# 44 runs of zero products at 22 distances between the addresses of the two operands, in place of thirteen forms

## The chip, the cores and the metric

The kernel runs on one core of one Trainium2 chip. The metric is the device time of one execution in microseconds (us); a nanosecond is written ns. The engines are called as the profile calls them: PE is TensorE's matmul side and PEld its weight loads, DVE is VectorE, ACT ScalarE, POOL GpSimd and SP SyncE. SBUF is the memory that the engines read, PSUM the one that PE writes, in banks of 512 fp32 columns on 128 partitions.

## The reference

Two networks in sequence work on 256 tokens of width 1024: first two layers of a modulated block (feed-forward, a mixer of neighbourhood attention and pooling, feed-forward) with a context stream beside them, then four layers of a second kind (a gated linear attention, a latent attention, a convolution and again the gated one, each followed by a squared-relu MLP and a gated per-layer term). Cut to what the end of the kernel computes:

```python
def second_block(x, p, ...):
    for i in range(DEPTH_2):
        ...
        x = layer_norm(ALPHA * x + h, ln_g[i, 0], ln_b[i, 0])
        x = layer_norm(ALPHA * x + sq_relu_mlp(x, mlp_w1[i], mlp_w2[i]), ln_g[i, 1], ln_b[i, 1])
        x = x + jax.nn.sigmoid(x @ ple_w_gate[i]) * (p[i] @ ple_w_proj[i])
    return x
```

The output is x, 1 x 256 x 1024 fp32. The probe, which is what the change rewrites, is no part of the reference: it multiplies zeros by zeros and its products are read by nobody.

## The kernel before, in words

`_program` builds a `Net` and calls `block1`, `block2` and `probe` one after the other; a scheduler then puts the instructions of each engine in an order, and waits on semaphores tie the engines together. Every weight is loaded once by SP's queue, split by ACT (L169, the rounded part `whi`, type fp32r) and DVE (L170, the rest, `wlo`), and each product is made of three matmuls into one PSUM bank: high by high (L180), high by low (L181, L182), so PE runs long sequences of matmuls of 512 or 256 columns. A matmul in the program is two instructions on PE: the load of the 128 x 128 weights (LDWEIGHTS, shown as PEld) and the matmul that streams the other operand past them.

The last stage of the network is `ple` in its last call. It multiplies x by the gate weights (tiles named `ple`, 128 x 512), ACT takes the sigmoid (L922, tile `sgm`), DVE multiplies by the projected term (L923) and adds into the rows (L924, tile `xr`), both in pieces of 256 columns, and SP sends each piece out (L926).

`probe` comes last in the program. It opens a pool of SBUF tiles and a pool of six PSUM banks. Four fp32r tiles `pra`, `prb`, `prc`, `pre` and two bf16 tiles `pru`, `prv`, each 128 x 1056, are set to zero by DVE (L1288). A helper `run` then issues n matmuls of one form into one bank or two (L1296), as one accumulation: the first starts it, the last ends it. There are thirteen forms, 276 matmuls: p0 to p3 shift either operand by 8 columns (32 bytes), p4 and p10 are bf16, p5 has 256 columns, p6 has 64 columns of weights, p7 two banks, p8 64 rows, p9 the two halves of the rows in turn, and p11 and p12 (24 each) go round two pairs of tiles and several places in each.

The pool takes memory that tiles of the network used before. So the memsets wait for the last readers of that memory, and the banks for the last readers of the banks. Waits follow the part of a tile that an instruction touches: a matmul waits for the memset of what it reads.

Of the kernel before, what the change touches and what calls it, by code (L numbers as in the profile page):

```python
# [8 lines left out]
F32 = mybir.dt.float32  # L9
F32R = mybir.dt.float32r  # L10
I32 = mybir.dt.int32
BF16 = mybir.dt.bfloat16
# [3 lines left out]
PSUM = bass.MemoryType.PSUM  # L16
DRAM = bass.MemoryType.DRAM

P = 128
# [79 lines left out]
class Net:  # L99
# [35 lines left out]
    def bank(self):  # L135
        return self.ps.tile([P, 512], F32, tag="bank", name=self.ph)
# [1140 lines left out]
    def probe(self):  # L1277

        nc = self.nc
        self.ph = "probe"  # L1280
        with ExitStack() as ctx:
            pool = lambda name, bufs, **k: ctx.enter_context(self.tc.tile_pool(name=name, bufs=bufs, **k))
            pp = pool("probe", 1)
            ps = pool("probe_ps", 6, space=PSUM)
            a, b, c, e = (pp.tile([P, 1056], F32R, name="pr" + n) for n in "abce")
            u, v = (pp.tile([P, 1056], BF16, name="pr" + n) for n in "uv")
            for t in (a, b, c, e, u, v):
                nc.vector.memset(t.bitcast(F32) if t.dtype == F32R else t, 0.0)  # L1288
            bank = lambda: ps.tile([P, 512], F32, tag="probe", name="probe")

            def run(name, n, lhs, rhs, out=None, banks=1):
                bs = [bank() for _ in range(banks)]
                for i in range(n):
                    o = bs[i % banks]
                    o = o if out is None else out(o)
                    nc.tensor.matmul(o, lhsT=lhs(i), rhs=rhs(i), start=i < banks, stop=i >= n - banks)  # L1296

            run("p0", 20, lambda i: a[:, 0:128], lambda i: c[:, 0:512])
            run("p1", 20, lambda i: a[:, 0:128], lambda i: c[:, 8:520])
            run("p2", 20, lambda i: a[:, 8:136], lambda i: c[:, 8:520])  # L1300
            run("p3", 20, lambda i: a[:, 8:136], lambda i: c[:, 0:512])
            run("p4", 20, lambda i: u[:, 0:128], lambda i: v[:, 0:512])
            run("p5", 24, lambda i: a[:, 8:136], lambda i: c[:, 8:264], out=lambda o: o[:, :256])
            run("p6", 20, lambda i: a[:, 8:72], lambda i: c[:, 8:520], out=lambda o: o[:64, :])
            run("p7", 20, lambda i: a[:, 0:128], lambda i: c[:, 0:512], banks=2)
            run("p8", 20, lambda i: a[:64, 0:128], lambda i: c[:64, 0:512])
            run("p9", 20, lambda i: a[64 * (i % 2):64 * (i % 2) + 64, 0:128],
                lambda i: c[64 * (i % 2):64 * (i % 2) + 64, 0:512], banks=2)
            run("p10", 24, lambda i: u[:, 0:128], lambda i: v[:, 0:256], out=lambda o: o[:, :256])
            run("p11", 24, lambda i: (a, b)[i % 2][:, 128 * (i % 8):128 * (i % 8) + 128],  # L1310
                lambda i: (c, e)[i % 2][:, 512 * (i // 2 % 2):512 * (i // 2 % 2) + 512])
            run("p12", 24, lambda i: (a, b)[i % 2][:, 8 + 128 * (i % 8):8 + 128 * (i % 8) + 128],
                lambda i: (c, e)[i % 2][:, 8 + 512 * (i // 2 % 2):8 + 512 * (i // 2 % 2) + 512])


_NAMES = [
# [40 lines left out]
```

## Time and profile before

| | us |
|---|---|
| median of the two timed runs | 3102.1 |
| lowest and highest of them | 3097.98, 3106.21 |
| the profiled execution, its own time | 3095.24 |
| its span, first to last instruction | 3093.5 |
| mean granted clock of TensorE in it | 0.997 of full |

The profile is of one execution. An engine's busy share counts its instructions and not its waits. A matmul's duration runs from its start to its modelled end; matmuls overlap in the pipeline, so a stretch of n of them is shorter than n durations. In a row of the timeline, equal instructions that follow each other are merged into one with their count; the duration is then from the first start to the last end. A few per cent of the matmul records can be missing.

### The profile page before, as it was taken

The page shows a single profiled execution, that of the slowest core. Times are in us where ns is not written, and L with a number is a line of the kernel's source. Part 1 is how long each engine was busy: PE and PEld are TensorE (multiplying, and loading weights), DVE is VectorE, ACT ScalarE, POOL GpSimd, SP SyncE. Part 2 cuts the span into 40 slices and gives each one's busy share as a digit, 9 for nine tenths or more (in the row PEclk, how much of TensorE's full clock was granted, in tenths as well). Part 3 has the DMA queues.
Part 4 walks back from the last instruction along what each step waited for, and adds up shares of the span by engine and source line. Part 5 has one row for each costly group of instructions (what it writes and reads, how often), then busy time and mean ns, then how long its engine had stood idle before and what let it go on. Part 6 is the DMA issues. An engine that isn't in the chain of part 4 may idle for free.

```text
span 3093.5 us, 41224 instructions
## 1 busy us (share of the span) xinstructions
PE 3028.1 (98%) x16637; PEld 2518.3 (81%) x16638; DVE 1880.7 (61%) x2460; ACT 1281.8 (41%) x1876; POOL 288.6 (9%) x480
## 2 busy tenths in 40 slices
PE   7999999999999999999999999999999999999999
PEld 5777777787778877877699779887988998788987
DVE  5657665577553875337755577566756765666651
ACT  3222235542222422225644555455544454465440
POOL 2101020010100200011100130010000000021000
PEclk9999999999999999999999999999999999999999
DMA  7545531345442454222446536553655565535550
GB/s 277 188 159 192 169 116 52 103 163 186 152 140 95 164 187 150 93 95 94 138 159 199 191 111 201 188 175 118 198 188 188 179 205 191 175 131 186 188 171 14
DMA packets 321939, 484.75 MB, mean 157 GB/s; under 512 B 16606, under 2 KB 199442, under 8 KB 320340
## 3 DMA queue, kind: packets, MB, share of 16 engines
q1 hardware_dynamic: 307844, 461.75, 45.3%
q0 software_dynamic: 9296, 16.16, 1.6%
q10 hardware_dynamic: 4608, 4.20, 0.5%
q8 instruction: 131, 2.15, 0.3%
q14 instruction: 60, 0.49, 0.0%
HBM read 480.97 MB, written 1.10 MB: 156 GB/s over the span
## 4 chain that ended last, share of the span: by engine, by line
PE 88%; DVE 5%; POOL 2%; ACT 2%; DMA 2%; issue 1%; SPq 0%; ACTq 0%; DVEq 0%; POOLq 0%
PE ffn_gu L180 9%; PE ffn_gu L182 9%; PE ffn_gu L181 9%; PE mlp L181 7%; PE mlp L182 7%; PE mlp L180 7%; PE ffn_dn L182 4%; PE ffn_dn L181 4%; PE ffn_dn L180 4%; PE m L180 2%; PE m L181 2%; PE m L182 2%; PE probe L1296 2%; DVE wlo L170 2%; PE mix_in L181 1%; PE mix_in L180 1%
## 5 line engine op out<-in xcount | busy, mean ns | idle before, releaser
L170 DVE TENSOR_TENSOR wlo<-raw,whi 128x1024 fp32r<-128x1024 f32 (+1 forms) x735 | 884.6, 1211 | 635.9 <-ACT whi L169 620.7
L169 ACT CAST whi<-raw 128x1024 fp32r<-128x1024 f32 (+1 forms) x735 | 760.8, 1038 | 1128.1 <-PE ffn_gu L181 292.9
L181 PE MATMUL ffn_gu<-hT_lo,whi 128*128 128x512 f32 (+1 forms) x1472 | 524.9, 357 | 1.8 <-DVE hT_lo L175 1.8
L180 PE MATMUL ffn_gu<-hT_hi,whi 128*128 128x512 f32 (+1 forms) x1472 | 525.0, 357 | 0.5 <-ACT hT_hi L174 0.5
L182 PE MATMUL ffn_gu<-hT_hi,wlo 128*128 128x512 f32 (+1 forms) x1472 | 524.2, 357 | 0.7 <-DVE wlo L170 0.7
L180 PEld LDWEIGHTS ffn_gu<-hT_hi,whi 128*128 128x128 f32 x1472 | 277.8, 189 | 52.9 <-ACT whi L169 4.2
L181 PEld LDWEIGHTS ffn_gu<-hT_lo,whi 128*128 128x128 f32 x1472 | 277.8, 189 | 43.9 <-DVE hT_lo L175 2.4
L182 PEld LDWEIGHTS ffn_gu<-hT_hi,wlo 128*128 128x128 f32 x1472 | 277.8, 189 | 43.9 <-DVE wlo L170 1.3
L347 DVE SCALAR_TENSOR_TENSOR macc<-raw,sil,macc 128x1024 f32<-128x1024 f32 x224 | 274.6, 1277 | 37.8 <-DMA raw<-in_w_mod_dram 37.8
L180 PE MATMUL mlp<-xT_hi,whi 128*128 128x256 f32 x896 | 253.9, 283 | 0.0
L181 PE MATMUL mlp<-xT_lo,whi 128*128 128x256 f32 x896 | 253.8, 283 | 0.0
L182 PE MATMUL mlp<-xT_hi,wlo 128*128 128x256 f32 x896 | 253.5, 283 | 0.0
L180 PE MATMUL ffn_dn<-whi,hid_hi 128*128 128x512 f32 x616 | 244.1, 396 | 0.0
L181 PE MATMUL ffn_dn<-wlo,hid_hi 128*128 128x512 f32 x616 | 243.6, 395 | 0.0
L182 PE MATMUL ffn_dn<-whi,hid_lo 128*128 128x512 f32 x616 | 243.5, 395 | 0.0
L180 PE MATMUL mlp<-whi,mlp_hi 128*128 128x512 f32 x512 | 199.2, 389 | 0.0
L181 PE MATMUL mlp<-wlo,mlp_hi 128*128 128x512 f32 x512 | 199.2, 389 | 0.0
L182 PE MATMUL mlp<-whi,mlp_lo 128*128 128x512 f32 x512 | 199.2, 389 | 0.0
L181 PEld LDWEIGHTS mlp<-xT_lo,whi 128*128 128x128 f32 x896 | 172.0, 192 | 0.0
L182 PEld LDWEIGHTS mlp<-xT_hi,wlo 128*128 128x128 f32 x896 | 172.0, 192 | 0.0
L180 PEld LDWEIGHTS mlp<-xT_hi,whi 128*128 128x128 f32 x896 | 172.0, 192 | 0.0
L180 PEld LDWEIGHTS ffn_dn<-whi,hid_hi 128*128 128x128 f32 x616 | 115.9, 188 | 29.4 <-ACT yrow L489 2.5
(414 smaller groups left out, 4889.8 us busy)
## 6 DMA issues: line engine op xcount, KB each, us to landing
raw<-in_mlp_w_dram SPq DMA_DIRECT2D x128, 1024.0 KB, 5.3
raw<-in_w_ffn_gate_up_dram SPq DMA_DIRECT2D x80, 1024.0 KB, 5.4
raw<-in_w_mod_dram SPq DMA_DIRECT2D x72, 1024.0 KB, 5.0
raw<-in_w_ffn_down_dram SPq DMA_DIRECT2D x32, 1024.0 KB, 5.1
raw<-in_gla_w_in_dram SPq DMA_DIRECT2D x24, 1024.0 KB, 5.2
raw<-in_w_in_dram SPq DMA_DIRECT2D x16, 1024.0 KB, 5.1
raw<-in_ple_w_gate_dram SPq DMA_DIRECT2D x16, 1024.0 KB, 5.1
raw<-in_w_ffn_down_dram SPq DMA_DIRECT2D x16, 768.0 KB, 4.6
```

The source lines that it names most:

```text
L169: self.nc.scalar.copy(hi, v)
L170: self.nc.vector.tensor_sub(lo, v, hi.bitcast(F32))
L180: mm(ps, lhsT=a[0], rhs=b[0], start=first, stop=False)
L181: mm(ps, lhsT=a[0], rhs=b[1], start=False, stop=False)
L182: mm(ps, lhsT=a[1], rhs=b[0], start=False, stop=last)
L347: nc.vector.scalar_tensor_tensor(acc[s], raw[:, k - k0, :], c, acc[s], ALU.mult, ALU.add)
L1296: nc.tensor.matmul(o, lhsT=lhs(i), rhs=rhs(i), start=i < banks, stop=i >= n - banks)
```

## The change

The body of `probe` is replaced. There is one fp32r tile `pra` of 128 x 26624 (106,496 bytes in each partition), set to zero by 13 memsets of 2048 columns, and a pool of four PSUM banks. The weights are always columns 0 to 127. The other operand begins 4096 + d bytes behind the beginning of the weights, for 22 values of d from 0 to 98304. At each d there is a run of 18 matmuls of 512 columns and a run of 20 matmuls of 256, each run one accumulation in a bank of its own, taken from the four in turn: 44 runs, 836 matmuls.

```diff
-            ps = pool("probe_ps", 6, space=PSUM)
-            a, b, c, e = (pp.tile([P, 1056], F32R, name="pr" + n) for n in "abce")
-            u, v = (pp.tile([P, 1056], BF16, name="pr" + n) for n in "uv")
-            for t in (a, b, c, e, u, v):
-                nc.vector.memset(t.bitcast(F32) if t.dtype == F32R else t, 0.0)
...
-            run("p0", 20, lambda i: a[:, 0:128], lambda i: c[:, 0:512])
...
-            run("p12", 24, lambda i: (a, b)[i % 2][:, 8 + 128 * (i % 8):8 + 128 * (i % 8) + 128],
-                lambda i: (c, e)[i % 2][:, 8 + 512 * (i // 2 % 2):8 + 512 * (i // 2 % 2) + 512])
+            ps = pool("probe_ps", 4, space=PSUM)
+            a = pp.tile([P, 26624], F32R, name="pra")
+            for o in range(0, 26624, 2048):
+                nc.vector.memset(a[:, o:o + 2048].bitcast(F32), 0.0)
+            low = (0, 16, 32, 64, 96, 128, 160, 192, 224, 256, 320, 384, 448)
+            high = (512, 1024, 2048, 4096, 8192, 16384, 32768, 65536, 98304)
+            for d in low + high:
+                m = (4096 + d) // 4
+                for n, count in ((512, 18), (256, 20)):
+                    b = ps.tile([P, 512], F32, tag="probe", name="probe")
+                    for i in range(count):
+                        nc.tensor.matmul(b[:, :n], lhsT=a[:, 0:P], rhs=a[:, m:m + n], start=i == 0, stop=i == count - 1)
```

On DVE, at the end of its program, the difference of the two orders reads as follows (L1341 and L1323 are the branch at the end; xN is a count of equal instructions):

```order
 L923 TENSOR_TENSOR sgm<-sgm,pe 128x256 x2
 L924 TENSOR_TENSOR xr<-xr,sgm 128x256 x2
-L1288 MEMSET pra 128x1056
 L923 TENSOR_TENSOR sgm<-sgm,pe 128x256 x2
 L924 TENSOR_TENSOR xr<-xr,sgm 128x256 x2
-L1288 MEMSET prb 128x1056
-L1288 MEMSET prc 128x1056
-L1288 MEMSET pre 128x1056
-L1288 MEMSET pru 128x528
-L1288 MEMSET prv 128x528
```

The memset of pra, which stood ahead of the network's last products and sums, is gone, and all memsets now stand behind these:

```order
+L1287 MEMSET pra 128x2048 x13
```

On PE, before, this is the passage from the network's last matmul to the probe, with the semaphores that are waited for (DVE_49 counts DVE's instructions, PE_49 PE's own, Activation_49 ACT's):

```order
L182 MATMUL ple_25273<-whi,xT_lo 128x512
L1296 MATMUL probe<-prc,pra 128x512 [waits DVE_49,PE_49,Activation_49]
L1296 MATMUL probe<-prc,pra 128x512 x79
L1296 LDWEIGHTS pru [waits DVE_49]
L1296 MATMUL probe<-prv,pru 128x512 [waits DVE_49]
```

And now, the same passage; behind it the runs go on in the same pattern, of 18 and of 20, each waiting for PE_49 when its bank is used again:

```order
L182 MATMUL ple_25273<-whi,xT_lo 128x512
L1295 MATMUL probe<-pra 128x512 [waits DMASW3_49,DMASW4_49,DMASW1_49,DMASW5_49,DMASW0_49,DMASW6_49,DVE_49,Activation_49]
L1295 MATMUL probe<-pra 128x512 x17
L1295 MATMUL probe<-pra 128x256 x20
L1295 MATMUL probe<-pra 128x512 x18
```

The run at d = 4096, the seventeenth distance, and the runs at 16384, 32768, 65536 and 98304 wait for DVE once more; the first of these reads so:

```order
L1295 MATMUL probe<-pra 128x256 x19
L1295 MATMUL probe<-pra 128x512 [waits DVE_49,PE_49]
L1295 MATMUL probe<-pra 128x512 x17
L1295 MATMUL probe<-pra 128x256 [waits PE_49]
L1295 MATMUL probe<-pra 128x256 x19
```

What moved: DVE's six memsets became thirteen, behind the last sums of the network, and PE's tail of thirteen forms became 44 runs that wait for parts of one tile. Nothing else moved on any engine.

## Rows read from the trace of the kernel before

**Rows 1.** The page: its head, busy time by engine, and the chain's summary.
```profile
span 3093.5 us, 41224 instructions
...
PE 3028.1 (98%) x16637; PEld 2518.3 (81%) x16638; DVE 1880.7 (61%) x2460; ACT 1281.8 (41%) x1876; POOL 288.6 (9%) x480
...
PE 88%; DVE 5%; POOL 2%; ACT 2%; DMA 2%; issue 1%; SPq 0%; ACTq 0%; DVEq 0%; POOLq 0%
```

**Rows 2.** Timeline, end of the network: start, duration, engine, line, operation [idle before <- releaser].
```profile
3028.98 0.39 PE L182 MATMUL ple<-whi,xT_lo 128*128 128x512 f32 x1
3029.40 0.66 ACT L922 ACTIVATE sgm<-ple 128x256 f32<-128x256 f32 x2 [4.78 <-PE ple L182]
3029.66 0.94 DVE L1288 MEMSET pra<- 128x1056 f32 x1 [3.85 <-PE ple L182]
3030.51 0.69 DVE L923 TENSOR_TENSOR sgm<-sgm,pe 128x256 f32<-128x256 f32 x2
3031.12 0.75 DVE L924 TENSOR_TENSOR xr<-xr,sgm 128x256 f32<-128x256 f32 x2
...
3032.04 0.94 DVE L1288 MEMSET prb<- 128x1056 f32 x1 [0.17 <-issue]
3033.15 0.94 DVE L1288 MEMSET prc<- 128x1056 f32 x1 [0.17 <-issue]
...
3034.26 0.94 DVE L1288 MEMSET pre<- 128x1056 f32 x1 [0.17 <-issue]
```

**Rows 3.** Timeline of PE in the probe, windows cut at its forms.
```profile
3034.23 5.43 PE L1296 MATMUL probe<-prc,pra 128*128 128x512 f32 x12 [4.87 <-DVE prc L1288]
...
3039.49 15.92 PE L1296 MATMUL probe<-prc,pra 128*128 128x512 f32 x68
...
3055.25 4.49 PE L1296 MATMUL probe<-prv,pru 128*128 128x512 bf16 x19
...
3059.39 3.21 PE L1296 MATMUL probe<-prc,pra 128*128 128x256 f32 x24
...
3075.23 3.56 PE L1296 MATMUL probe<-prc,pra 64*128 64x512 f32 x25
...
3081.59 0.39 PE L1296 MATMUL probe<-pre,prb 128*128 128x512 f32 x1
...
3092.11 0.40 PE L1296 MATMUL probe<-pre,prb 128*128 128x512 f32 x1
```

**Rows 4.** Stretches by engine: length, busy us (count), then PEclk, DMA share, GB/s.
```profile
3034.20:3039.50 5.30, 5.27 (x13) 4.14 (x14) 1.93 (x3) 0.00 (x0) 0.00 (x0) 0.50 0.01 3
3039.50:3055.20 15.70, 15.70 (x69) 12.58 (x67) 0.00 (x0) 0.00 (x0) 0.00 (x0) 1.00 0.00 0
...
1538.30:1544.40 6.10, 4.40 (x19) 4.10 (x20) 3.64 (x7) 1.60 (x5) 1.57 (x2) 0.50 0.53 172
...
20.30:27.00 6.70, 4.32 (x20) 0.53 (x24) 0.75 (x1) 1.15 (x2) 0.80 (x2) 1.00 1.01 418
```

**Rows 5.** Timeline of PE: the first matmul after two other idle times.
```profile
1538.30 0.58 PE L180 MATMUL ffn_gu<-whi,hT_hi 128*128 128x256 f32 x1 [3.81 <-ACT hT_hi L174]
...
20.22 1.93 PE L323 MATMUL mod<-raw,sil 128*32 128x512 f32 x8 [2.59 <-DMA raw<-in_w_mod_dram]
```

**Rows 6.** Stretches of the network: mlp at 256 and 512 columns, ffn_gu at 512 and 256.
```profile
1881.00:1960.00 79.00, 79.00 (x661) 79.00 (x660) 49.84 (x55) 42.10 (x54) 0.00 (x0) 1.00 0.60 190
1961.00:2047.00 86.00, 86.00 (x381) 71.19 (x380) 43.51 (x42) 34.32 (x34) 1.70 (x2) 1.00 0.54 180
1228.00:1332.00 104.00, 104.00 (x449) 84.34 (x448) 35.37 (x39) 28.31 (x36) 1.92 (x4) 1.00 0.31 99
1557.00:1606.00 49.00, 49.00 (x415) 49.00 (x414) 27.79 (x35) 22.92 (x35) 0.00 (x0) 1.00 0.61 197
```

**Rows 7.** Line L1296: count, duration in ns (min/median/max), first and last start.
```profile
L1296 PE MATMUL probe<-prc,pra x208: 278/390/767, 3034.2 to 3091.9; 128*128 128x512 f32 x62, 64*128 64x512 f32 x20, 128*128 128x256 f32 x12, 128*64 128x512 f32 x10
L1296 PEld LDWEIGHTS probe<-pre,prb x24: 187/188/192, 3081.4 to 3091.9; 128*128 128x128 f32 x24
```

More of the change, by code (lines that the diff above doesn't have):

```diff
@@ L1283, in probe @@
             pp = pool("probe", 1)
-            ps = pool("probe_ps", 6, space=PSUM)
-            a, b, c, e = (pp.tile([P, 1056], F32R, name="pr" + n) for n in "abce")
-            u, v = (pp.tile([P, 1056], BF16, name="pr" + n) for n in "uv")
-            for t in (a, b, c, e, u, v):
-                nc.vector.memset(t.bitcast(F32) if t.dtype == F32R else t, 0.0)
[L1289 to L1296, printed above, removed]
@@ L1298, in probe @@
-            run("p0", 20, lambda i: a[:, 0:128], lambda i: c[:, 0:512])
[L1299 to L1311, printed above, removed]
```

## The prediction

> **What bounds the kernel now.** I read the page's head, its busy shares and the summary of the chain first, to see which engine sets the end: the span is 3093.5 us, PE is busy for 98% of it and the chain that ended last lies on PE for 88% [rows 1]. The probe is the last thing that PE does, and nothing is left to run beside it: once its matmuls have begun, each one more is paid in full. So the question is narrow: how long the old probe stands at the end, and how long the new one will.
>
> Then the timeline where the network ends and the probe begins [rows 2, 3]. The last matmul of the network starts at 3028.98. PE then waits 4.87 us until the first probe matmul at 3034.23, and the releaser that is named is the memset of prc, the third on DVE. Ahead of it on DVE stand the memset of pra, the two last products and sums of the network (L923, L924) and the memset of prb. From 3034.23 to the start of the last matmul, 3092.11, and its end 0.40 later, the old probe takes 58.3 us [rows 3]; 1.0 us is left from there to the end of the span [rows 1, 3].
>
> Third, the clock by stretches [rows 4]. After the 4.87 us in which PE did nothing, the granted clock is 0.50 over the probe's first 5.3 us (the lower level, 1.2 GHz), and 1.00 from then on. An idle time of 3.81 us, near 1538 us, was followed by the same, 0.50 for 6.1 us; one of 2.59 us near the start of the program was not: the clock stood at 1.00 behind it [rows 4, 5].
>
> Last, how far apart matmuls start when they follow each other without a wait. The mean duration of a matmul does not tell this, since they are pipelined (390 ns in the median [rows 7], at starts some 230 ns apart); a merged row's length less one duration, divided by its count less one, does, and so does a long stretch in which PE is busy all the time, divided by its count.
>
> **The change part by part.** It takes out 276 matmuls in thirteen forms and puts in 22 x 18 = 396 matmuls of 512 columns and 22 x 20 = 440 of 256, all fp32r, 128 rows by 128 columns of weights, full array. Every other instruction of the five engines stands where it stood, so the network itself is priced at nothing, before and after. Only the end moves.
>
> Price of 512 columns. The trace does not show all 22 distances, but it shows many pairs of addresses. In the old probe's first four forms, at full clock, 68 matmuls take 15.92 us: (15.92 - 0.39) / 67 = 231.8 ns each. In its last two forms 47 matmuls have 46 intervals from 3081.59 to 3092.11, 228.7 ns each [rows 3]. In the network, 381 in 86 us are 225.7 ns and 449 in 104 us are 231.6 ns [rows 6] (a window counts one or two that were in flight at its edge, under 1%). So operands at hundreds of different distances stay within 226 to 232 ns. I take 228.7, the value of a probe with changing addresses: 396 x 0.2287 = 90.6 us, between 89.4 and 91.8.
>
> Price of 256 columns. 661 in 79 us are 119.5 ns and 415 in 49 us are 118.1 ns [rows 6]; 24 of the old probe take 3.21 us, (3.21 - 0.28) / 23 = 127.4, with a slow start behind bf16 in it [rows 3]. I take 119.5, from the longest stretch: 440 x 0.1195 = 52.6 us, between 52.0 and 56.1. Together 143.2 us, bounds 141.4 to 147.9. Changing the bank between runs is in this at no cost: each run waits only for the bank of four runs earlier, and the old probe went from form to form inside the row of 68 without a visible break.
>
> The start. DVE now has 13 memsets of 2048 elements, all behind the network's last sums instead of between them. The old ones start 1.11 us apart for 1056 elements (3032.04, 3033.15, 3034.26) [rows 2], 1.05 ns an element, so 2.15 us for 2048 and 28 us for all. The order shows one wait for DVE on the first probe matmul and further ones where the runs at 4096, 16384, 32768, 65536 and 98304 begin. So the first needs the first memset alone, and the others run under matmuls: the last is done some 28 us after the first began, and its readers come some 137 us after the first matmul. Without pra's memset ahead of them, L923 and L924 end about 0.6 us earlier than 3031.87 [rows 2], the memset begins near 3031.3, and PE starts at about 3033.5, 0.7 us before 3034.23. If it began at 3032.04 as prb's did, PE would start at 3034.2, no gain; 0 to 1 us are the bounds.
>
> The clock. PE then stands idle for 4.1 us, between the 3.81 and the 4.87 that were each followed by the lower level. In the old probe the first 12 matmuls took 3039.49 - 3034.23 = 5.26 us where 12 x 0.2318 = 2.78 would have done [rows 3]: 2.5 us lost. I charge the same again. At no drop it would be 0; with 6.1 us at the lower level, 6.1 / 0.438 = 14 matmuls that need 3.2 us otherwise, 2.9.
>
> The sum, against the profiled execution's own time. Start 3033.5, plus 143.2, plus 2.5, plus 0.2 for the last matmul to drain (0.28 against 0.12) is 3179.4, against 3092.5: +86.9 us. Onto its own 3095.24 that is 3182.1. The median of the two timed runs, 3102.1, lies 6.9 above that execution, and the higher of them, 3106.2, another 4.1; onto the median it gives 3189.0. I predict 3187 us, nearer to the median since that is what is compared. Bounds: +82.6 with the cheapest matmuls and no loss to the clock, +92 with the dearest; on 3095.2 to 3106.2 this spans 3178 to 3198.
>
> A rule of the Trainium skill would make the price another. The row first: fp32r starts 226 to 232 ns apart at 512 columns, while the old probe's bf16 form, 20 of 512 columns of which one record is missing, takes 4.49 us, (4.49 - 0.38) / 19 = 216 ns [rows 3]. The Trainium skill, "TensorE: Matmul & The Clock Gate", section Back-to-back issue gap, gives N/2.4 + 2.5 ns for the gap from one matmul to the next, 215.8 and 109.2 ns here whatever the addresses; by it the sum would be an estimate of 133.5 us in place of 143.2, ten less. The bf16 row agrees with it and no fp32r row does, so I stay with the rows.
>
> **The rivals.**
> First, some distances collide. Where they do, the load of the weights cannot run under the matmul ahead of it. A load takes 188 ns [rows 7]; unhidden it would add 38 x 0.188 = 7.1 us per distance. For it: one tile holds both operands now, and the far distances, up to 98304 bytes, are tried on purpose in no row. Against: in the network operands lie that far apart too, and no stretch of [rows 6] is slower than 232. With the nine distances of the second list it is +64, 3251 us; with three of them +21, 3208.
>
> Second, the other side, not slower: matmuls that run beside each other. Two that use different halves of the rows do: 25 of 512 columns take 3.56 us, (3.56 - 0.39) / 24 = 132 ns apart [rows 3]. If repeated products with the same weights into one bank overlapped in the same way, the new probe would take 396 x 0.132 + 440 x 0.066 = 81 us, +23, and end at 3125, within 2% of before. It decides from a mean of 144 ns per matmul on (58.3 + 62 us over 836), where I expect 171. Against: the first forms of the old probe are just that, the same weights into one bank on all 128 rows, and go at 231.8 [rows 3]. The section of the Trainium skill named above also gives some 131 ns per matmul for a sustained stream of pairs of load and matmul at N = 512 and 81 at N = 128; with 98 taken between them, an estimate by that page is 95 us, +39, 3141, and no stretch of [rows 6] agrees with it.
>
> Third, the first matmul waits for the whole tile, all 13 memsets. Then PE starts 12 x 2.15 = 25.8 us later: 3213 us. The separate waits at the far distances speak against it.
>
> That the change doesn't do what it says (no distance stands out, all 22 alike) is within the forecast: it moves the time by under 3 us.
>
> **How the numbers follow.** Forecast 0.88, collisions 0.05, overlap 0.04, a late start 0.03. About 2% (62 us) is what a measurement of this kernel can tell from no change; +87 is 2.8%, and its bounds, 83 to 92, lie outside. Slower by over 2%: the forecast, the collisions and the late start, less 0.01 for a body that happens to run faster, 0.95. Within 2%: 0.04. Faster: 0.01. The range 3176 to 3200 takes the bounds of the sum with 2 us on either side, and leaves out the rivals' 0.12.
>
> **What would show it right or wrong.** The page of the changed kernel should have 836 probe matmuls in some 146 us; runs of 18 at 226 to 232 ns and of 20 at 118 to 120, at every distance; a granted clock of 0.50 for 5 to 6 us behind a PE idle time of some 4 us, and 1.00 after; one memset of about 2 us ahead of the first matmul, twelve beside the rest; the network's last matmul near 3029. A run with starts 300 ns apart or more shows a collision, a PE idle time of 28 us the late start, and runs at 130 the overlap.

## The result, and the profile after

The changed kernel takes 3187.3 us (median of two runs, 3184.67 and 3190.01) against 3102.1 before: a ratio of 1.0275, with a 95% interval from 1.0205 to 1.0344. It is slower, by 85 us. The forecast was 3187 us, in a range of 3176 to 3200.

The page of the changed kernel, its head, the busy time by engine, the chain's summary and the row of the probe, against [rows 1]:

```profile
span 3182.9 us, 42361 instructions
...
PE 3117.5 (98%) x17198; PEld 2603.4 (82%) x17198; DVE 1898.3 (60%) x2467; ACT 1281.9 (40%) x1876; POOL 290.6 (9%) x480
...
PE 89%; DVE 4%; ACT 2%; POOL 2%; DMA 1%; issue 1%; ACTq 0%; SPq 0%; POOLq 0%; DVEq 0%
...
L1295 PE MATMUL probe<-pra 128*128 128x256 f32 (+1 forms) x836 | 146.1, 338 | 4.3 <-issue 4.3
```

PE is busy 89.4 us longer than before and the span is 89.4 us longer (2.1 of it by the network's own later end, below): all that was added is on the path, as a tail with nothing beside it must be. ACT and POOL are within 2 us of what they were. The mean of 338 ns in the last row mixes both widths and is again a duration, not a price: 146.1 us over 836 matmuls is 175 ns.

The timeline where the network ends and the probe begins, against [rows 2] and the first row of [rows 3]. Columns: start, duration, engine, line, operation, and in brackets the idle time before it:

```profile
3031.10 0.39 PE L182 MATMUL ple<-whi,xT_lo 128*128 128x512 f32 x1
3035.79 0.77 PE L1295 MATMUL probe<-pra 128*128 128x512 f32 x1 [4.30 <-issue]
...
3031.94 0.76 DVE L923 TENSOR_TENSOR sgm<-sgm,pe 128x256 f32<-128x256 f32 x2 [4.01 <-ACT sgm L922]
3032.62 0.75 DVE L924 TENSOR_TENSOR xr<-xr,sgm 128x256 f32<-128x256 f32 x2
3033.92 1.76 DVE L1287 MEMSET pra<- 128x2048 f32 x1 [0.55 <-issue]
3036.06 1.76 DVE L1287 MEMSET pra<- 128x2048 f32 x1 [0.38 <-issue]
...
3059.61 1.76 DVE L1287 MEMSET pra<- 128x2048 f32 x1 [0.37 <-issue]
```

The network's last matmul starts at 3031.10, 2.1 us later than in the trace of before; no instruction of the network differs, and this is scatter (the last section). PE is idle for 4.30 us, where 4.1 were expected. One memset stands ahead of the first matmul, which starts 1.87 us after it. The memsets start 2.14 us apart, and the twelve others, up to the one at 3059.61, lie beside matmuls.

The stretches of the probe (length, busy time and count of PE, PEld, DVE, ACT, POOL, then granted clock, DMA share, GB/s), against [rows 4]:

```profile
3035.79:3040.89 5.10, 5.10 (x12) 4.04 (x13) 4.08 (x3) 0.00 (x0) 0.00 (x0) 0.50 0.01 3
3040.90:3181.80 140.90, 140.90 (x825) 124.51 (x824) 17.09 (x10) 0.00 (x0) 0.00 (x0) 1.00 0.00 1
```

The lower level, 1.2 GHz, holds for the first 5.1 us, as before the change, and 2.4 GHz from there to the end. Last, the timeline of PE inside four runs and at the end, against [rows 3]: d = 320 at 512 and at 256 columns, d = 1024 at 512, d = 8192 at 256, and the last run.

```profile
3104.08 3.90 PE L1295 MATMUL probe<-pra 128*128 128x512 f32 x16
...
3108.05 2.17 PE L1295 MATMUL probe<-pra 128*128 128x256 f32 x17
...
3130.92 3.11 PE L1295 MATMUL probe<-pra 128*128 128x512 f32 x13
...
3153.60 2.20 PE L1295 MATMUL probe<-pra 128*128 128x256 f32 x17
...
3180.32 1.60 PE L1295 MATMUL probe<-pra 128*128 128x256 f32 x12
```

Length less one duration, over the count less one: (3.90 - 0.39) / 15 = 234 ns at d = 320 and (3.11 - 0.39) / 12 = 227 at d = 1024; at 256 columns (2.17 - 0.28) / 16 = 118 and (2.20 - 0.28) / 16 = 120. So the distance tells, a little, and the other way round at the two widths. From the starts of all matmuls, the runs of 512 after the first have means from 226.6 to 233.9 ns, 230.5 over all; those of 256 from 116.8 to 120.2, 118.9 over all. No distance comes near the 300 ns that would have shown a collision.

### The profile page after: what moved, and what is told of

Read it like the earlier page. It is cut to its first block, busy times and chain, and to the rows that moved or that the text cites. A ratio compares the mean times of both kernels' runs of the same rounds, so it can differ in the third digit from the quotient of the medians.

```text
span 3182.9 us, 42361 instructions
## 1 busy us (share of the span) xinstructions
PE 3117.5 (98%) x17198; PEld 2603.4 (82%) x17198; DVE 1898.3 (60%) x2467; ACT 1281.9 (40%) x1876; POOL 290.6 (9%) x480
## 4 chain that ended last, share of the span: by engine, by line
PE 89%; DVE 4%; ACT 2%; POOL 2%; DMA 1%; issue 1%; ACTq 0%; SPq 0%; POOLq 0%; DVEq 0%
PE ffn_gu L180 9%; PE ffn_gu L182 9%; PE ffn_gu L181 9%; PE mlp L181 7%; PE mlp L182 7%; PE mlp L180 7%; PE probe L1295 5%; PE ffn_dn L182 4%; PE ffn_dn L181 4%; PE ffn_dn L180 4%; PE m L180 2%; PE m L181 2%; PE m L182 2%; DVE wlo L170 2%; PE mix_in L181 1%; PE mix_in L180 1%
## 5 line engine op out<-in xcount | busy, mean ns | idle before, releaser
L1295 PE MATMUL probe<-pra 128*128 128x256 f32 (+1 forms) x836 | 146.1, 338 | 4.3 <-issue 4.3
```

Source lines behind the costliest of these rows:

```text
L1295: nc.tensor.matmul(b[:, :n], lhsT=a[:, 0:P], rhs=a[:, m:m + n], start=i == 0, stop=i == count - 1)
```

## The experiments

Theory: the probe is a tail in which every matmul is paid in full, 146 us behind a network that the change does not touch, with one memset ahead and some 2.5 us lost to the clock. The rivals are those of the prediction. Each kernel is the changed one with the edit shown; `...` stands for lines left out. The kernel before took 3102.3 us in the median of the eight runs beside the first four experiments.

**The network alone.**

```diff
         net.block2()
-        net.probe()
```

> The probe is left out; the network is whole. Theory (the end is paid in full): from the changed kernel's trace the end moves from 3182.9 to the landing of the last output, issued at 3033.5 with 0.4 us of issue and 1.7 us to landing, so about 3035.6; that is 147.3 us less, a time of about 3040 us, 62 below the kernel before (ratio 0.980), and the network's last matmul near 3029 to 3031 as in both. Rival (a part of the probe lies beside something at the end that stays): less than 55 us gained over the kernel before.

Measured: 3039.3 us, ratio to before 0.9798 (0.9783 to 0.9814). The end of its timeline, PE's last matmul and the issue of the last outputs:

```profile
3035.73 0.39 PE L182 MATMUL ple<-whi,xT_lo 128*128 128x512 f32 x1
...
3037.70 0.82 SPq L926 DMA_DIRECT2D out_dram<-xr  x2
```

Behind the last matmul come 2.4 us of sums and of issuing the outputs, and their landing. The new probe costs 3187.3 - 3039.3 = 148 us over the network alone (147.3 expected), the old one 63. To within the scatter of the network's end, nothing of either is hidden. This kernel computes the same outputs and is the faster one of the three.

**A small memset first.**

```diff
-            for o in range(0, 26624, 2048):
+            for o, n in ((0, 128), (1024, 512), (128, 896), (1536, 512)):
+                nc.vector.memset(a[:, o:o + n].bitcast(F32), 0.0)
+            for o in range(2048, 26624, 2048):
```

> Against the changed kernel: the first memset of 2048 columns is cut into four, and the 640 columns that the first run reads come first (0.14 + 0.53 us in place of 1.87 until PE is released). Theory (the idle time decides the lower clock, as 3.81, 4.30 and 4.87 us did and 2.5 to 2.8 us did not): PE idle about 3.1 us in place of 4.30, no or less of the lower level, 1.2 us from the earlier start and up to 2.5 us of the clock, so a probe of 143.6 us in place of 146.1. Rival (the clock falls at any such end of the network): only the 1.2 us, the first 12 matmuls still 427 ns apart, and the probe 146 us or a little more.

Measured: 3191.2 us, ratio 1.0274 (1.0246 to 1.0303), not told apart from the changed kernel. Its first matmuls, its stretches, and the same two views of a matmul near the start of the program:

```profile
3043.79 2.90 PE L1297 MATMUL probe<-pra 128*128 128x512 f32 x6 [2.95 <-issue]
...
3040.85:3043.79 2.94, 0.00 (x1) 0.04 (x1) 2.16 (x7) 0.66 (x2) 0.00 (x0) 0.99 0.14 48
3043.79:3046.65 2.86, 2.86 (x7) 2.28 (x8) 2.43 (x3) 0.00 (x0) 0.00 (x0) 0.50 0.15 48
3046.70:3188.80 142.10, 142.10 (x829) 125.50 (x829) 19.91 (x12) 0.00 (x0) 0.00 (x0) 1.00 0.00 1
...
7.10 1.94 PE L323 MATMUL mod<-raw,sil 128*32 128x512 f32 x8 [3.20 <-DMA raw<-in_w_mod_dram]
...
7.10:9.10 2.00, 1.93 (x8) 0.20 (x8) 0.00 (x0) 0.00 (x0) 0.48 (x1) 1.00 0.97 391
```

PE is idle for 2.95 us in place of 4.30, and the clock falls all the same, but only 7 matmuls are slow in place of 12: 2.86 - 7 x 0.23 = 1.3 us lost in place of 5.10 - 12 x 0.23 = 2.3. Neither expectation holds as it was put. The length of the idle time alone does not decide whether the clock falls: in this trace it fell after 2.95 us and stood at 1.00 after 3.20 us near the start of the program, where PE had run one small matmul. Nor does it decide how long the lower level lasts. The kernel with one operand in turn (below) has nearly the idle time of the changed one, and its clock rises as early as here:

```profile
3043.45 2.90 PE L1294 MATMUL probe<-pra 128*128 128x512 f32 x6 [4.29 <-issue]
...
3043.45:3045.90 2.45, 2.45 (x6) 1.97 (x7) 1.80 (x2) 0.00 (x0) 0.00 (x0) 0.50 0.03 7
```

So the 1 us of clock that this trace gained over the changed kernel's is no more than such traces differ by, and is not shown to come from the smaller memset; the 1.35 us of idle time does. In the same trace the network ends 9.4 us later than in the changed kernel's, which hides both.

**The far distances first.**

```diff
-            for d in low + high:
+            for d in (low + high)[::-1]:
```

> Against the changed kernel: the 22 distances in reverse order, so that the first run reads what the last memset writes. Theory (the first matmul waits for the memset of what it reads, and the others were hidden): PE idle 4.3 + 12 x 2.14 = 30 us, the start 25.7 us later, the probe 146 us as before, so about 3213 us, ratio to the kernel before 1.036. Rival (the first matmul waited for the whole tile in any order, or the memsets cost nothing): the time of the changed kernel, 3187.

Measured: 3211.0 us, ratio 1.0347 (1.0329 to 1.0366). The first matmul in its timeline, and the stretch after:

```profile
3058.08 0.77 PE L1295 MATMUL probe<-pra 128*128 128x512 f32 x1 [30.09 <-issue]
```

```profile
3058.08:3061.20 3.12, 3.12 (x7) 2.45 (x8) 0.00 (x0) 0.00 (x0) 0.00 (x0) 0.50 0.02 5
3061.30:3203.00 141.70, 141.70 (x829) 125.09 (x828) 0.00 (x0) 0.00 (x0) 0.00 (x0) 1.00 0.00 1
```

30.09 us idle in place of 4.30: 25.8 us, the time of twelve memsets, which the changed kernel's order of the runs has under matmuls. That was the price of the third rival, and the waits on parts of the tile are what spared it. The lower level lasts for some 3 us here, after 30 us without work, and for 5.1 in the changed kernel, after 4.3.

**Half of the rows.**

```diff
-                    b = ps.tile([P, 512], F32, tag="probe", name="probe")
+                    b = [ps.tile([P, 512], F32, tag="probe", name="probe") for _ in range(2)]
                     for i in range(count):
-                        nc.tensor.matmul(b[:, :n], lhsT=a[:, 0:P], rhs=a[:, m:m + n], start=i == 0, stop=i == count - 1)
+                        r = slice(64 * (i % 2), 64 * (i % 2) + 64)
+                        nc.tensor.matmul(b[i % 2][:, :n], lhsT=a[r, 0:P], rhs=a[r, m:m + n],
+                                         start=i < 2, stop=i >= count - 2)
```

> Against the changed kernel: each matmul takes 64 of the 128 rows, the two halves in turn, each into its own bank; half of each product is left out. Theory (matmuls on all rows follow each other, those on different halves run beside each other): 132 and 66 ns per matmul, 396 x 0.132 + 440 x 0.066 = 81 us and a little for the clock, so about 3123 us, ratio about 1.007. Rival (the matmul's price is its columns, whatever the rows): 146 us and 3187.

Measured: 3118.7 us, ratio 1.0051 (1.0034 to 1.0068). The first matmuls of its probe and the last, and the stretch from the end of the first run on:

```profile
3043.62 0.79 PE L1296 MATMUL probe<-pra 64*128 64x512 f32 x2 [4.30 <-issue]
...
3115.93 1.12 PE L1296 MATMUL probe<-pra 64*128 64x256 f32 x15
...
3047.00:3116.70 69.70, 69.70 (x820) 64.02 (x818) 18.45 (x11) 0.00 (x0) 0.00 (x0) 1.00 0.01 1
```

836 matmuls in 73.4 us, half of the 146: this is what the second rival would have looked like, down to a time within 2% of before. In the changed kernel no run shows it. The 81 us expected came from a row of 25 in which a few single matmuls stood beside the pairs.

**All rows and half of them in turn.**

```diff
+                        r = slice(0, 128 - 64 * (i % 2))
-                        nc.tensor.matmul(b[:, :n], lhsT=a[:, 0:P], rhs=a[:, m:m + n], start=i == 0, stop=i == count - 1)
+                        nc.tensor.matmul(b[:, :n], lhsT=a[r, 0:P], rhs=a[r, m:m + n], start=i == 0, stop=i == count - 1)
```

> Against the changed kernel: matmuls on all 128 rows and on the first 64 rows in turn, into one bank; part of each product is left out. It measures a weight load that cannot run under the matmul ahead of it, the price in the first rival. By the prediction's price, the whole load of 188 ns: starts 415 and 308 ns apart, a probe of 396 x 0.415 + 440 x 0.308 = 300 us. By the nearest row of the old probe, 318 ns at the one change from 128 to 64 rows: 318 and 210 ns, 218 us. If the load is still hidden: 146 us.

Measured in a single execution: 3555.2 us beside 3104.8 for the kernel before. None of the three values is near: the probe takes 511 us. One stretch of it, and the weight loads:

```profile
3300.00:3400.00 100.00, 100.00 (x163) 46.24 (x163) 0.00 (x0) 0.00 (x0) 0.00 (x0) 0.50 0.00 0
```

```profile
L1296 PEld LDWEIGHTS probe<-pra x836: 284/286/288, 3041.5 to 3551.8; 128*128 128x128 f32 x84, 64*128 64x128 f32 x84
```

A matmul starts every 613 ns in the mean; from the starts, 723 at 512 columns and 510 at 256. The clock fell at the idle time ahead of the probe, as in the other kernels, and did not rise again in 511 us, although PE counts as busy throughout. So two causes were mixed in one number, the load and the clock.

**The same behind matmuls at the upper level.**

```diff
-            for d in low + high:
+            for k, d in enumerate(low + high):
...
+                        half = k >= 11 and (i // (4 if k < 17 else 1)) % 2
+                        r = slice(0, 64 if half else 128)
...
```

> Three parts in place of one: 11 distances as in the changed kernel, then 6 with four matmuls on 128 rows and four on 64 in turn, then 5 with 128 and 64 in turn one by one; part of the products is left out. It asks what a load that is not hidden costs at the full clock, and whether a clock at its upper level falls behind such matmuls. If the run before stayed slow only because it began at the lower level: the clock stays at 1.00 in all three parts, and a change of rows costs about 91 to 108 ns there (the old probe's 318 and 335), the third part 190 x 0.170 + 19 = 51 us. If matmuls with such gaps bring the clock down by themselves: 0.50 in the third part, 723 and 510 ns as in the run before, 90 x 0.723 + 100 x 0.510 = 116 us.

A single execution, 3270.6 us. The stretches: the first run of the second part, the first run of the third, and the rest of the third; then the timeline of the first run of the third part, and a window of 0.36 us inside it with the weight loads.

```profile
3108.64:3113.40 4.76, 4.76 (x20) 2.87 (x19) 0.00 (x0) 0.00 (x0) 0.00 (x0) 1.00 0.00 0
3157.32:3164.90 7.58, 7.58 (x20) 3.21 (x18) 0.00 (x0) 0.00 (x0) 0.00 (x0) 1.00 0.00 0
3165.80:3268.00 102.20, 102.04 (x170) 48.53 (x170) 0.00 (x0) 0.00 (x0) 0.00 (x0) 0.50 0.00 0
```

```profile
3157.32 7.69 PE L1297 MATMUL probe<-pra 128*128 128x512 f32 x18
...
3158.50 0.18 PEld L1297 LDWEIGHTS probe<-pra 64*128 64x128 f32 x1 [0.25 <-issue]
3158.50 0.93 PE L1297 MATMUL probe<-pra 64*128 64x512 f32 x2
3158.93 0.19 PEld L1297 LDWEIGHTS probe<-pra 128*128 128x128 f32 x1 [0.25 <-issue]
```

In fours the clock stays up, and each change of rows lengthens two gaps, the one up to the matmul on the new rows and the one behind it: over the whole second part, 315 to 342 ns at 512 columns where the others are 228 to 241. The two together are 196 ns over the price without a change in the mean, at 512 columns and at 256. One by one, the first run stands at 1.00, and its starts behind the first two are 420 to 432 ns apart, 429 in the mean; the first gap at 256 columns is 315. That is 196 and 197 ns over the second part's price without a change (232.6 and 117.9). So a change of rows costs the same in both parts, close to the whole load of 188 ns [rows 7] that the prediction charged; the 91 to 108 ns expected here had counted one gap of the two. The window shows why: the load on 64 rows starts with the matmul that needs it, at 3158.50, and not under the matmul ahead. A matmul's record here holds the time of its load, and its end is modelled, so a PE that counts as busy is not one that streams all the time.

Then the clock falls to 0.50, behind matmuls that follow each other with such gaps and with next to no idle time in the record, and stays there: 102.2 us for 170. So the second expectation held, and the first rival's price was right for the load alone and left out the clock. Half rows in turn and changes in fours both ran at 1.00; what in the turn one by one brings the clock down was not taken apart.

**Which distance it is.** Three kernels ask whether the small effect hangs on the distance or on the places. First, both operands moved together, at d = 0, 256 and 320:

```diff
...
-            for d in low + high:
-                m = (4096 + d) // 4
+            for s, d in [(s, d) for d in (0, 256, 320) for s in (0, 8, 16, 32, 48, 64, 96)]:
+                m = s + (4096 + d) // 4
...
-                        nc.tensor.matmul(b[:, :n], lhsT=a[:, 0:P], rhs=a[:, m:m + n], start=i == 0, stop=i == count - 1)
+                        nc.tensor.matmul(b[:, :n], lhsT=a[:, s:s + P], rhs=a[:, m:m + n],
+                                         start=i == 0, stop=i == count - 1)
```

> 21 pairs in place of the 22 distances: d = 0, 256 and 320, and at each of them both operands moved together by 0, 32, 64, 128, 192, 256 and 384 bytes. If the distance modulo 512 bytes sets the price: 226.6 to 227.4 ns at 512 columns and 120.0 at 256 for d = 0 and 256 in all 14 places, 233.4 and 117.8 for d = 320 in all seven. If the place of the streamed operand (or of the weights) modulo 512 sets it: the values change along the seven places of one distance, and d = 320 moved by 192 looks like d = 0.

A single execution, 3177.1 us with 38 matmuls fewer. Runs at d = 320, moved by 64 and by 128 bytes at 512 columns, by 128 and by 192 at 256:

```profile
3142.09 4.05 PE L1293 MATMUL probe<-pra 128*128 128x512 f32 x17
...
3148.57 4.13 PE L1293 MATMUL probe<-pra 128*128 128x512 f32 x17
...
3152.66 2.40 PE L1293 MATMUL probe<-pra 128*128 128x256 f32 x19
...
3159.13 2.32 PE L1293 MATMUL probe<-pra 128*128 128x256 f32 x19
```

228.8 and 233.8 ns, 117.8 and 113.3, at one distance. At d = 0 and 256 all places give 226.6 to 228.3 once a run has settled (from its fourth gap on) and the clock is up, and 120.0. At d = 320 six of the seven places give 228.6 to 229.3 and one 233.4. So at 256 columns the distance separates its multiples of 256 from 320, and at 512 columns it hardly does here: neither expectation holds whole. The two places do not decide either. The pair of places with no move, at d = 320, took 234 ns in the changed kernel, above; the same pair in the kernel with the far distances first:

```profile
3131.62 3.83 PE L1295 MATMUL probe<-pra 128*128 128x512 f32 x16
```

That is 229 ns, and 230 in this kernel. Between the changed kernel and that with the far distances first only the order of the runs differs, and with it the bank of each, so one of these has a part in it; which was not tried.

Then the whole map, in steps of 64 bytes:

```diff
...
-            for d in low + high:
-                m = (4096 + d) // 4
+            for s, t in [(16 * s, 16 * t) for s in range(8) for t in range(8)]:
+                m = 1024 + t
...
-                        nc.tensor.matmul(b[:, :n], lhsT=a[:, 0:P], rhs=a[:, m:m + n], start=i == 0, stop=i == count - 1)
+                        nc.tensor.matmul(b[:, :n], lhsT=a[:, s:s + P], rhs=a[:, m:m + n],
+                                         start=i == 0, stop=i == count - 1)
```

> 64 pairs in place of the 22 distances: weights 0 to 448 bytes on in steps of 64, the streamed operand 4096 bytes further and 0 to 448 on in steps of 64, every combination, 1216 matmuls; about 70 us more than the changed kernel. If the distance modulo 512 alone sets the price: the 64 values are the same along each line of equal distance, 227 and 120 ns on the lines 0 and 256, 229 to 233 and 118 on the others. If the places count: they differ along a line, as 229 and 233 did at 320 when both operands were moved.

A single execution, 3457.7 us. The expected count is wrong: 64 pairs are 2432 matmuls, and the time is 270 us above the changed kernel's for 1596 more of them, 169 ns each. Mean gaps of settled runs (again from the fourth gap on), by distance modulo 512, worked out from the starts of all matmuls in the trace; the very first run, at the lower clock, is left out of the first column of numbers:

```
distance      512 columns                     256 columns
0, 256        226.6 or 226.7, once 228.3      120.0, once 120.2
128, 384      232.4                           118.4 to 120.0
64, 192,      233.3 or 233.4 (three of 32:    117.8 (nine of 32: 113.3
320, 448      228.6 to 228.9)                 or 113.4)
```

In this kernel the price at 512 columns follows the distance modulo 256 bytes, nearly whatever the places. At odd multiples of 64 bytes a run can settle into a second, cheaper pattern, as most did in the kernel with both operands moved, and which of the two it takes is explained neither by the distance nor by the places.

Third, two operands in turn, so that a matmul's distance to its own weights and to those of the next differ:

```diff
+            same, own, cross = ((0, 1024), (256, 1024)), ((0, 1024), (336, 1104)), ((0, 1104), (336, 1024))
+            for pair in (same, own, cross) * 7:
...
+                        s, m = pair[i % 2]
...
```

> Two weights and two streamed operands in turn, three kinds of runs, seven times each. Kind one: all distances a multiple of 512 bytes. Kind two: the distance of each matmul to its own weights is a multiple of 512, the one to the weights of the next matmul is 192 or 320 off. Kind three: the own is 192 or 320 off, the one to the next a multiple. If the stream of a matmul meets the load of the next one's weights: 227 and 120 ns for kinds one and three, 233.4 and 117.8 for kind two. If the own distance counts: 227 and 120 for kinds one and two, 233.4 and 117.8 for kind three.

A single execution, 3181.3 us. A run of kind two, of kind three, and of kind one, at 512 columns:

```profile
3067.43 4.10 PE L1294 MATMUL probe<-pra 128*128 128x512 f32 x17
...
3073.97 4.12 PE L1294 MATMUL probe<-pra 128*128 128x512 f32 x17
...
3080.55 4.04 PE L1294 MATMUL probe<-pra 128*128 128x512 f32 x17
```

231.9, 233.1 and 228.1 ns: both mixed kinds are dear (at 256 columns 118.3 and 119.2, between the two values expected), so the run does not tell the own weights from the next. With one operand in turn only:

```diff
+            streams, weights = ((0, 1024), (0, 1104)), ((0, 1024), (336, 1024))
+            for pair in (streams, weights) * 11:
...
```

> Two kinds of runs, eleven times each: the same weights with two streamed operands in turn (0 and 320 off modulo 512), and two weights in turn (0 and 336 columns, 320 off the other way) with the same streamed operand. If each matmul is priced by the one distance between its stream and the weights loaded beside it: both kinds take the mean of 227 and 233.4, 230 ns at 512 columns, and 119 at 256. If the change of the operand itself costs, as the 231.6 and 233.1 of both mixed kinds before may mean: 232 or more in both.

```profile
3051.60 4.12 PE L1294 MATMUL probe<-pra 128*128 128x512 f32 x17
...
3058.15 4.09 PE L1294 MATMUL probe<-pra 128*128 128x512 f32 x17
```

A single execution, 3191.7 us. The first row, weights in turn, gives 233.1 ns and the second, streams in turn, 231.3; settled, 232.1 and 231.3. The first expectation, 230 in both, does not hold, and the second, 232 or more in both, does for the weights alone. What in the distance costs the 6 ns stays open.

**The same distances in bf16.**

```diff
-            a = pp.tile([P, 26624], F32R, name="pra")
-            for o in range(0, 26624, 2048):
-                nc.vector.memset(a[:, o:o + 2048].bitcast(F32), 0.0)
+            a = pp.tile([P, 53248], BF16, name="pra")
+            for o in range(0, 53248, 4096):
+                nc.vector.memset(a[:, o:o + 4096], 0.0)
...
-                m = (4096 + d) // 4
+                m = (4096 + d) // 2
```

> The changed kernel's distances in bytes, with both operands bf16. If the price is that of the streamed columns alone, as the old probe's bf16 form had it: 216 ns at 512 columns and 109 at 256 at all 22 distances, a probe of 133.5 us and some 2.5 for the clock. If the distance tells in bf16 too: a step of some 6 ns between the distances that are multiples of 256 bytes and the others.

A single execution, 3172.7 us. Two runs, at d = 128:

```profile
3066.86 3.62 PE L1295 MATMUL probe<-pra 128*128 128x512 bf16 x16
...
3070.75 2.02 PE L1295 MATMUL probe<-pra 128*128 128x256 bf16 x17
```

(3.62 - 0.38) / 15 = 216 ns and (2.02 - 0.27) / 16 = 109. From the starts, 215.8 and 109.2 at all 22 distances once the clock is up (15 of the 836 records are missing, and the gaps across them are left out). The gap rule of the Trainium skill, "TensorE: Matmul & The Clock Gate", section Back-to-back issue gap, N/2.4 + 2.5 ns, is met to the digit here. The changed kernel's fp32r runs pay 11 to 18 ns more at 512 columns.

## Why the prediction was right, point by point

The sum was made as start, matmuls, clock, drain. The matmuls of 512 columns cost 230.5 ns where 228.7 was taken from the last two forms of the old probe, those of 256 columns 118.9 where 119.5 was taken: 396 x 0.2305 + 440 x 0.1189 = 143.6 us against 143.2. The first run's gaps have a mean of 372.9 ns, so the clock took (372.9 - 230.5) x 17 = 2.4 us against 2.5. That these two agree so well is in part luck: worked out in the same way, other kernels lost from 1.4 us (one operand in turn) to 2.6 (the map) after the same idle time of 4.3 us. With the drain the probe is 146.1 us long, against 145.9. Reading the price from starts and not from durations was the step that carried it.

The start was 3035.79, not 3033.5. Of the 2.3 us, 2.1 are the network's own end, and 0.2 the rest: the memset began 0.5 us later behind PE's end than worked out, and released PE after 1.87 us and not 2.15, two errors that cancel in part. The span came out at 3182.9 against 3180.4 mainly for that reason. Placing the forecast between the profiled execution's own time plus the sum and the median plus the sum was a choice, and that it met 3187.3 to the microsecond is luck: the two runs of the changed kernel lie 5.3 us apart, and the network's end scatters by more (the last section).

The rivals: no distance collides, and the dearest settled price in the map, 233.4 ns, is 7 above the cheapest. The overlap happens on half rows only (73.4 us), and its price had been set 10% too high; of the two sums for it, the +39 holds 2.5 us for the clock and the +23 leaves them out. The late start is real, 25.8 us, where the order of the runs asks for it. What a load costs that is not hidden had been set at 188 ns and measured 196 to 197 at the upper clock; that matmuls with such a load each bring the clock down was not foreseen.

## What to carry to other kernels

Price a stream of matmuls by the gaps between starts in a stretch without waits, form by form; durations say little. Work at the very end of a program is paid in full, so its size can be read from the rows of its own form, and the few microseconds around it, an idle time and a clock that has to rise again, from the rows at its beginning; the clock's part is known to a microsecond or so. A probe that measures needs a whole run behind the clock's rise, and its parts in an order that lets the preparation of the far ones lie under the near ones.

## What had not been expected of the hardware

Matmuls on 128 and on 64 rows in turn brought the granted clock from 1.00 to 0.50 and kept it there, with PE busy nearly all the time in the record, though that counts the loads: 723 and 510 ns a matmul, against 230 and 119.

The network's end scatters by 13 us between traces of kernels whose network is the same instruction for instruction, from 3028.0 to 3040.8 us. A stretch in the middle tells the two groups apart, here the changed kernel and the one with the small memset first:

```profile
2105.00:2140.00 35.00, 32.86 (x184) 24.01 (x182) 24.69 (x94) 21.88 (x59) 0.00 (x0) 1.00 0.31 105
```

```profile
2105.00:2140.00 35.00, 33.17 (x156) 24.74 (x154) 21.75 (x67) 20.23 (x42) 0.00 (x0) 0.79 0.31 106
```

In five of thirteen traces the clock in it is 0.76 to 0.79, and in those the network ends between 3036 and 3041; in the other eight it is 1.00, and the end lies between 3028 and 3034. What makes the clock fall there in some executions was not tried.
